# A hybrid decoder block on one core: half of w_out split earlier, the last unit's o written into loaded tiles, a wait of VectorE, and a new layout of the projection's input

## The chip, the cores and the metric

The kernel runs on one core of one Trainium2 chip. The metric is the device time of one execution in microseconds; lower is better. Several runs are made, and their median is given.

## The reference, cut to what matters

One layer, sequence 1024, model width 1024, everything in float32:

```python
mod = silu(c) @ w_ada + b_ada                      # six vectors of 1024: shift, scale, gate, twice
h = rms_norm(x, g_attn_pre) * (1 + sc_a) + sh_a
proj = h @ w_in
qa, ka, qb, kb = partial_rope(...)                 # parts of proj; va, vb without it
oa = banded_attention(qa, ka, va, 127, sink)       # 8 query heads, 2 key heads, width 64
ob = dilated_mixture_attention(qb, kb, vb)         # 8 heads; windows (128,1), (512,4), (2048,16)
mixed = concat(rms_norm(oa, g_mix_a), rms_norm(ob, g_mix_b))
x = x + gt_a * rms_norm(mixed @ w_out, g_attn_post)
h = rms_norm(x, g_mlp_pre) * (1 + sc_m) + sh_m
x = x + gt_m * rms_norm(square(relu(h @ w_up)) @ w_down, g_mlp_post)    # width 4096
```

## The kernel before

**Precision.** Every operand of a large matmul is split into a high part (float32r, made by a ScalarE copy) and a low part (the difference, made by VectorE or GpSimd). A product is three matmuls: high by high, high by low, low by high. A step of a product (128 deep, 512 wide) is therefore three lines of matmuls in the profile.

**Stages.** First the modulation and the normalised, transposed input h^T, which is split into the tile `hw`, of shape [128, 8, 2, 1024]: 8 slots, 2 parts (high, low), 1024 columns. Then six units of projection (`proj_tile`, `proj_mm`, L866 to L869; unit 0 in `first_unit` with its own order, the tiles are then called `acc`): units 0 and 1 are the two key groups of mixer A, units 2 to 5 two heads of mixer B each. A unit has two halves x of 512 tokens and three column groups c; each of these 36 tiles is 8 steps over k. `evac` rotates and splits q and k into staging tiles named `hl` and stores them by DMA into `qt` and `kt`. Beside the projection runs attention over 48 items (`emit_item`): for units 0 and 1 one item for each of 8 query blocks, for units 2 to 5 one for each of 4 pairs of query blocks (tp) and each of two heads. An item is scores (`s_ps`), a masked minimum on VectorE, an exponential on ScalarE, a scaling on GpSimd (L1158), transposes (`pt_ps`), a split (`ph`) and the product with v (`o_ps`). Its o goes through `otmp` and `ot` (L1294, L1298) to DRAM (`o_dram`, L1301).

**Output projection.** `load_wo` loads the eight 128-row pieces of w_out into staging tiles `wo_st` and splits them into the slots of `hw`, which the projection's input has left: ScalarE the high part (L1353), VectorE (L1356) or GpSimd (L1361 and L1362) the low one. A slot holds all k of one block of 128 tokens, so slots 0 to 3 are free after the last tile of half 0 (u = 5, x = 0, c = 2), and slots 4 to 7 after the very last projection tile. `open_out` then gives the memory of the projection's pools to a ring `ring_l`. `out_block(tb)` handles 128 tokens: it loads o (`o_sb`, L1423) when all items of its pair are stored, splits it (`oh`, `ol`), forms the two norms, multiplies by w_out (`y_ps`, L1478 to L1480; 16 steps of three matmuls), norms, gates, adds x (loaded at L1427) and stores the residual stream (`x_dram`). A second norm follows (`norm(2, e)`: VectorE L1515, GpSimd's power L1517, ScalarE L1532), then the transposes `px` (L1541) and their copies into `h2` with the modulation (L1557, L1560). `norm(0, e)` is the first norm of the block, with the same code. x can be loaded only once attention's pools have been closed (`open_h2`).

**MLP.** From the blocks of `h2`, w_up and w_down are multiplied in halves by a scheme with seven products where eight would be usual. Sums and differences of quarters are made by VectorE, and every operand is split by ScalarE and VectorE (L1669, L1676). Its matmuls are L1912 to L1914.

**What sets the order of the work.** The program is written out by a planner in the kernel, `Sched`. Every operation has an engine, an estimated duration, events that it depends on and resources that it takes and gives (`Res`: counts of free buffers, such as `r_stg` for five staging tiles, `r_wo` for the free slots of `hw`). `Sched.run` always emits the operation that could start first by these estimates; `prio` breaks ties, and for TensorE a list of preferences does (attention ahead of `dense` work, once the projections are done). The result is one fixed order for each engine and one for SP's DMA queue. On the chip each engine keeps to its order and waits on semaphores, whatever the true durations are. `feed_...` functions hand work to the planner when a condition holds: `feed_out` hands over block tb when 42 + 2 * (tb // 2) items of attention are done and at most ten steps of dense work are queued. `st.d` counts units of projection done.

## Time and profile before

| | us |
|---|---|
| median of 3 runs | 1146.05 |
| lowest and highest run | 1145.21, 1146.7 |
| the profiled execution, its own time | 1144.1 |
| its span, first to last instruction | 1142.2 |
| TensorE busy in it | 1113.5 (97%) |
| VectorE, ScalarE, GpSimd busy | 819.3, 636.1, 267.8 |

The profiled execution is a run of its own, and its time is not among the three. PE is TensorE's matmuls, PEld its weight loads, DVE VectorE, ACT ScalarE, POOL GpSimd, SP the queue that issues the DMAs. A row of a timeline gives the start and the duration in us, engine, line, operation, tiles (written <- read), shape, count, and in brackets the idle time of the engine before it with what ended it. Matmuls overlap, so their pace is read from their starts. "Granted clock" is the share of TensorE's full clock.

### The profile page before, as it was taken

Reading aid. Unit: us, or ns where it says so; the run is one execution under the profiler, and the core shown is the slowest. Engines: PE = TensorE matmul, PEld = TensorE weight load, DVE = VectorE, ACT = ScalarE, POOL = GpSimd, SP = SyncE. Lnnn points to the kernel's source line nnn. Section 1 sums busy time; section 2 is a strip of 40 time slices with the busy share of each in tenths; the row PEclk is TensorE's granted clock in tenths of the full one; section 3 lists DMA queues with packets and bytes.
Section 4 is the critical chain, followed back from the end, with each engine's and each line's share of the span. In section 5 each row is a group of like instructions: output and inputs, shape, how many; then the busy total and the mean of one; then the engine's idle time right before and its main releaser. Section 6 shows DMA issues by size and latency. Waiting matters only on the chain.

```text
span 1142.2 us, 15600 instructions
## 1 busy us (share of the span) xinstructions
PE 1113.5 (97%) x5417; PEld 925.2 (81%) x5417; DVE 819.3 (72%) x1378; ACT 636.1 (56%) x1101; POOL 267.8 (23%) x349
## 2 busy tenths in 40 slices
PE   8999999999999899998999999999999999999996
PEld 7788878888888687887888888888888888888885
DVE  7878666666667766668879664599644896537998
ACT  8868865464556755676675434553244733246542
POOL 2458867565743521112000000000000000000002
PEclk9999999999999899999999999999999999999998
DMA  9565545343423305555780168712469112584103
GB/s 351 187 208 164 164 155 168 136 155 125 141 77 133 127 26 186 185 202 217 284 310 19 56 230 292 280 41 70 152 245 331 55 56 86 202 304 164 37 19 148
DMA packets 90910, 185.29 MB, mean 162 GB/s; under 512 B 8400, under 2 KB 31056, under 8 KB 90832
## 3 DMA queue, kind: packets, MB, share of 16 engines
q1 hardware_dynamic: 90832, 184.30, 46.1%
q8 instruction: 43, 0.70, 0.2%
q14 instruction: 35, 0.29, 0.1%
HBM read 137.08 MB, written 28.31 MB: 145 GB/s over the span
## 4 chain that ended last, share of the span: by engine, by line
PE 77%; DVE 8%; ACT 4%; issue 4%; POOL 3%; DMA 3%; SPq 0%; DVEq 0%; POOLq 0%; ACTq 0%
PE mlp_ps L1913 17%; PE mlp_ps L1914 17%; PE mlp_ps L1912 17%; PE pj L866 4%; PE pj L869 4%; PE pj L867 4%; PE s_ps L1127 3%; PE o_ps L1262 2%; PE y_ps L1478 1%; PE pt_ps L1232 1%; PE y_ps L1479 1%; PE y_ps L1480 1%; PE pt_ps L1235 1%; DMA o_sb<-o_dram 1%; PE o_ps L1267 1%
## 5 line engine op out<-in xcount | busy, mean ns | idle before, releaser
L1912 PE MATMUL mlp_ps<-hw 128*128 128x512 f32 x896 | 349.8, 390 | 0.0
L1913 PE MATMUL mlp_ps<-hw 128*128 128x512 f32 x896 | 348.8, 389 | 0.0
L1914 PE MATMUL mlp_ps<-hw 128*128 128x512 f32 x896 | 348.8, 389 | 0.0
L1912 PEld LDWEIGHTS mlp_ps<-hw 128*128 128x128 f32 x896 | 168.5, 188 | 35.5 <-issue 0.5
L1913 PEld LDWEIGHTS mlp_ps<-hw 128*128 128x128 f32 x896 | 168.4, 188 | 35.2 <-issue 0.5
L1914 PEld LDWEIGHTS mlp_ps<-hw 128*128 128x128 f32 x896 | 168.4, 188 | 34.9
L1676 DVE TENSOR_TENSOR hw<-w,hw 128x1024 fp32r<-128x1024 f32 x96 | 114.7, 1222 | 95.5 <-ACT hw L1669 95.2
L1669 ACT CAST hw<-w 128x1024 fp32r<-128x1024 f32 x96 | 97.7, 1047 | 128.1 <-PE mlp_ps L1914 97.5
L2012 POOL TENSOR_TENSOR st<-st,nhalf 128x1 f32<-128x1 f32 x8 | 7.8, 977 | 598.5 <-DVE st L2010 598.5
L866 PE MATMUL pj<-hw,w_hl 128*128 128x512 f32 x240 | 102.9, 429 | 0.0
L869 PE MATMUL pj<-hw,w_hl 128*128 128x512 f32 x240 | 95.1, 396 | 0.0
L867 PE MATMUL pj<-hw,w_hl 128*128 128x512 f32 x240 | 94.9, 395 | 0.0
L1250 DVE TENSOR_TENSOR ph<-pt_ps,ph 128x512 fp32r<-128x512 f32 (+1 forms) x110 | 69.5, 648 | 32.9 <-ACT ph L1246 32.6
L1669 ACT CAST hw<-u 128x1024 fp32r<-128x1024 f32 x48 | 48.6, 1051 | 64.6 <-PE mlp_ps L1914 64.6
L1246 ACT CAST ph<-pt_ps 128x512 fp32r<-128x512 f32 (+1 forms) x110 | 59.0, 556 | 31.2 <-PE pt_ps L1235 26.1
L1153 ACT ACTIVATE p_sb<-p_sb,mn 128x128 f32<-128x128 f32 (+3 forms) x64 | 49.7, 777 | 38.7 <-DVE mn L1146 37.2
L1676 DVE TENSOR_TENSOR hw<-u,hw 128x1024 fp32r<-128x1024 f32 x48 | 57.1, 1221 | 18.2 <-ACT hw L1669 18.2
L1970 DVE TENSOR_TENSOR yacc<-yacc,mlp_ps 128x512 f32<-128x512 f32 x96 | 62.3, 685 | 3.3 <-PE mlp_ps L1914 3.3
L1158 POOL TENSOR_SCALAR p_sb<-p_sb,den 128x128 f32<-128x128 f32 (+3 forms) x64 | 48.6, 765 | 55.4 <-DVE den L1156 50.8
L1015 POOL TENSOR_TENSOR ada_acc<-ada_acc,wa_st 128x512 f32<-128x512 f32 x42 | 54.9, 1307 | 3.5
L869 PEld LDWEIGHTS pj<-hw,w_hl 128*128 128x128 f32 x240 | 45.4, 189 | 10.6
L1478 PE MATMUL y_ps<-hw,oh 128*128 128x512 f32 x128 | 52.0, 406 | 0.0
(206 smaller groups left out, 2015.8 us busy)
## 6 DMA issues: line engine op xcount, KB each, us to landing
hw<-s_dram SPq DMA_DIRECT2D x84, 512.0 KB, 4.2
wa_st<-in_w_ada SPq DMA_DIRECT2D x32, 512.0 KB, 4.3
w<-in_w_up SPq DMA_DIRECT2D x32, 512.0 KB, 4.9
w<-in_w_down SPq DMA_DIRECT2D x32, 512.0 KB, 7.0
s_dram<-hw SPq DMA_DIRECT2D x28, 512.0 KB, 3.4
qt<-hl SPq DMA_DIRECT2D x40, 256.0 KB, 2.6
w_st<-in_w_in SPq DMA_DIRECT2D x36, 256.0 KB, 2.9
x_sb<-in_x SPq DMA_DIRECT2D x16, 512.0 KB, 6.5
```

The source lines that it names most:

```text
L866: T.matmul(ps, w[:, 0, n], h[0], start=(k == 0), stop=False)
L867: T.matmul(ps, w[:, 1, n], h[0], start=False, stop=False)
L869: T.matmul(ps, w[:, 0, n], h[1], start=False, stop=(k == KC - 1))
L1246: A.copy(b["ph"][:, 0, :w], b["pt"][:, :w])
L1250: V.tensor_tensor(b["ph"][:, 1, :w], b["pt"][:, :w], b["ph"][:, 0, :w].bitcast(F32), ALU.subtract)
L1478: T.matmul(ps[:], b["oh"][:, k], wh[:, c0:c0 + 512], start=(k == 4 * m), stop=False)
L1669: A.copy(out[j][0], flat(src[j]))
L1676: V.tensor_tensor(out[j][1], flat(src[j]), out[j][0].bitcast(F32), ALU.subtract)
L1912: T.matmul(ps[m][:], sh, mh, start=starts and k == 0, stop=False, **kw)
L1913: T.matmul(ps[m][:], sh, ml_, start=False, stop=False, **kw)
L1914: T.matmul(ps[m][:], sl, mh, start=False, stop=k == 3, **kw)
L1970: e = op("DVE", t_dv(512), lambda: V.tensor_tensor(y(), y(), ps[m][:], ALU.add), [e, ml.e_y[tb, n]], gives=gives, prio=1)
```

## The change

Five edits:

- **Layout of `hw` in the projection** (`mod_chunk`, `proj_mm`): slot 4 * x + k // 2 holds the two k of a pair for the 512 tokens of half x, side by side. The moving operand of a projection matmul is then 512 elements in a row; before it was four pieces of 128 from four slots. The last tile of each half gives back one slot after each second k (`r_wo`, 1), not all four at its end.
- **Half of w_out split earlier** (`split_wo`, `feed_wo`): pieces k = 4 to 7 are loaded, split by ScalarE and VectorE into two staging tiles and stored to DRAM (`wo_dram`) when the projection stands at 2.2, 3.0, 3.8 and 4.6 units. `load_wo` splits k = 0 to 3 as before, but with VectorE alone, and loads both parts of k = 4 to 7 from DRAM into `hw`, 1 MB in two DMAs for each slot that comes free.
- **The last unit's o of blocks 0 and 1** (`open_out`, `t_pv`, `out_block`): seven of the eight o rows of both blocks are loaded as soon as `ring_l` is open, and VectorE writes the o of items (5, 0, 0) and (5, 0, 1) into the eighth row of these tiles, in two operations of 64x128 for each item. These two items are no longer stored to DRAM.
- **VectorE waits** (`norm`): for the second norm of the last block, the mean on VectorE, GpSimd's power and a copy of its result by VectorE are one operation of the planner on VectorE, so VectorE stands still until the power is done. For the blocks before the last two the planner's estimate of the power is 0.55 us, not 1.2.
- **Queue** (`feed_out`): a block is handed over when at most 17 steps of dense work are queued, not 10. `t.a` becomes the dictionary `h2` itself, so that quarters that are made later are found in it.

```diff
--- before.py
+++ after.py
@@ -677,8 +677,8 @@
     def mod_chunk(k, eg, half):
         t0, t1 = (0, TB) if half is None else (4 * half, 4 * half + 4)
         n = (t1 - t0) * P
-        ks = slice(k * P, (k + 1) * P)
-        h, hh = xnT[:, k, t0 * P:t1 * P].rearrange("p (b t) -> p b t", t=P), hw[:, t0:t1, 0, ks]
+        h = xnT[:, k, t0 * P:t1 * P].rearrange("p (x t) -> p x t", t=512)
+        hh, hl = (hw[:, t0 // 4 * 4 + k // 2:t1 - 3 + k // 2:4, i, k % 2 * 512:k % 2 * 512 + 512] for i in range(2))
         deps = [eg] + (e_xn[0] + e_xn[1] if half is None else e_xn[half])
 
         def full(eng):
@@ -689,7 +689,7 @@
         eh = op("ACT", t_sb(n) + 2 * AP_COST, lambda: A.activation(hh, h, AF.Identity, bias=s_a[:, k:k + 1],
                                                                   scale=g_a[:, k:k + 1]), deps, prio=0)
         e = op("ACT", t_sb(n) + 2 * AP_COST, full(A), [eh], prio=0)
-        e = op("DVE", t_dv(n), lambda: V.tensor_tensor(hw[:, t0:t1, 1, ks], h, hh.bitcast(F32), ALU.subtract), [e],
+        e = op("DVE", t_dv(n), lambda: V.tensor_tensor(hl, h, hh.bitcast(F32), ALU.subtract), [e],
                prio=0)
         for x in (0, 1) if half is None else (half,):
             e_hh[k, x], e_hl[k, x] = eh, e
@@ -858,10 +858,9 @@
 
     def proj_mm(ps, u, c, k, x, part):
         i, n = w_at(u, c, k)
-        t, w = slice(k * P, (k + 1) * P), w_hl[u, i]
-        n = slice(n * P, n * P + P)
-        h = [hw[:, 4 * x:4 * x + 4, i, t] for i in range(2)]
-        ps = ps[:].rearrange("p (b t) -> p b t", t=P)
+        w, n = w_hl[u, i], slice(n * P, n * P + P)
+        h = [hw[:, 4 * x + k // 2, i, k % 2 * 512:k % 2 * 512 + 512] for i in range(2)]
+        ps = ps[:]
         if part != 1:
             T.matmul(ps, w[:, 0, n], h[0], start=(k == 0), stop=False)
             T.matmul(ps, w[:, 1, n], h[0], start=False, stop=False)
@@ -927,8 +926,8 @@
             gives = []
             if x and k % 4 == 3:
                 gives.append((r_w, 1))
-            if u == 5 and c == 2 and k == KC - 1:
-                gives.append((r_wo, 4))
+            if u == 5 and c == 2 and k % 2:
+                gives.append((r_wo, 1))
             d = dense(0.681, emit, [w_e[u, w_at(u, c, k)[0]]], takes=[(r_pj, 1)] if k == 0 else [], gives=gives, after=tick)
         evac(u, x, c, lambda: b[0], d, r_pj)
 
@@ -1072,6 +1071,10 @@
         return ada.i == NADA
 
 
+    NSTG2 = 4
+    ph2 = Tok()
+    ph2.ot, ph2.e_ot, ph2.e_lo = {}, [Ev(), Ev()], {}
+
     items = [(u, qb) for u in range(2) for qb in range(TB)]
     items += [(u, tp, h) for u in range(2, 6)
               for tp, h in ((0, 0), (0, 1), (1, 0), (1, 1), (2, 0), *(((3, 0), (2, 1)) if u < 5 else ((2, 1), (3, 0))), (3, 1))]
@@ -1297,6 +1300,13 @@
                 ob["ot"] = opool.tile([64, 512], F32, name="ot", tag="ot")[:, :256]
                 V.tensor_tensor(ob["ot"][:], rec.o[0:64, :256], ob["tmp"][:, :256], ALU.add)
             e = op("ACT", t_ps(256), f_o1, [ep], takes=[(r_tmp, 1)], prio=0)
+            if (u, tp) == (5, 0):
+                def f_o3():
+                    for j in range(2):
+                        c = slice(P * j, P * j + P)
+                        V.tensor_tensor(ph2.ot[j][64 * h:64 * h + 64, KC - 1], rec.o[0:64, c], ob["tmp"][:, c], ALU.add)
+                e_o[i] = op("DVE", 2 * t_dv(P), f_o3, [e, *ph2.e_ot], gives=[(r_ob, 1), (r_tmp, 1)], prio=0)
+                return
             e = op("DVE", t_dv(256), f_o2, [e], takes=[(r_ot, 1)], gives=[(r_ob, 1), (r_tmp, 1)], prio=0)
             e_o[i] = load(lambda: nc.sync.dma_start(o_dram[tp][2 + u, 64 * h:64 * h + 64], ob["ot"][:]), 65536, [e],
                           gives=[(r_ot, 1)], prio=-5)
@@ -1333,16 +1343,46 @@
         return next_item[0] == len(items)
 
 
-    NSTG2 = 4
-    ph2 = Tok()
+    wo_dram = [[dram.tile([P, 1024], F32, name=f"wo_dram{k}_{i}") for i in range(2)] for k in range(4, KC)]
+    e_wod = {}
+
+    def split_wo(k):
+
+        raw, hi = [], []
+        g = cols[:, 56 + k:57 + k]
+
+        def f_l():
+            raw.append(stage("wo_st"))
+            nc.sync.dma_start(raw[0][:], w_out[k * P:(k + 1) * P])
+        e = load(f_l, 524288, takes=[(r_stg, 1)], prio=21)
+
+        def f_h():
+            hi.append(stage("wo_hi"))
+            A.mul(hi[0][:].bitcast(F32R), raw[0][:], g)
+        eh = op("ACT", t_sb(D) + AP_COST, f_h, [e], takes=[(r_stg, 1)], prio=9)
+
+        def f_lo():
+            V.scalar_tensor_tensor(raw[0][:].bitcast(F32R), raw[0][:], g, hi[0][:], ALU.mult, ALU.subtract)
+        el = op("DVE", t_dv(D) + AP_DV, f_lo, [eh], prio=9)
+        e_wod[k] = [load(lambda t=t, i=i: nc.sync.dma_start(wo_dram[k - 4][i][:], t[0][:]), 524288, [e_],
+                         gives=[(r_stg, 1)], prio=22) for i, (t, e_) in enumerate(((hi, eh), (raw, el)))]
+
+    def feed_wo():
+        k = 4 + len(e_wod)
+        if st.d > WO_AT[k - 4]:
+            split_wo(k)
+        return len(e_wod) == 4
+
+    WO_AT = (2.2, 3.0, 3.8, 4.6)
+    sc.launch.append(feed_wo)
 
     def load_wo():
 
-        if len(todo_dense) > 2 or ada.i < NADA:
+        if len(todo_dense) > 2 or ada.i < NADA or len(e_wod) < 4:
             return False
         ph2.e_wo, ph2.raw = {}, {}
         eh = None
-        for k in range(KC):
+        for k in range(4):
             def f_l(k=k):
                 ph2.raw[k] = stage("wo_st")
                 nc.sync.dma_start(ph2.raw[k][:], w_out[k * P:(k + 1) * P])
@@ -1356,12 +1396,12 @@
                 V.scalar_tensor_tensor(hw[:, k, 1], ph2.raw[k][:], g, hw[:, k, 0].bitcast(F32), ALU.mult,
                                        ALU.subtract)
             eh = op("ACT", t_sb(D) + AP_COST, f_h, [e] + ([eh] if eh else []), prio=4)
-
-            def f_lo2(k=k, g=g):
-                G.tensor_scalar(ph2.raw[k][:], ph2.raw[k][:], g, 1.0, ALU.mult, ALU.mult)
-                G.tensor_tensor(hw[:, k, 1], ph2.raw[k][:], hw[:, k, 0].bitcast(F32), ALU.subtract)
-            ph2.e_wo[k] = op(("DVE", "POOL"), (t_dv(D) + AP_DV, t_pts(D) + t_ptt(D)), (f_lo, f_lo2), [eh],
-                             gives=[(r_stg, 1)], prio=4)
+            ph2.e_wo[k] = op("DVE", t_dv(D) + AP_DV, f_lo, [eh], gives=[(r_stg, 1)], prio=4)
+        for k in range(4, KC):
+            def f_d(k=k):
+                for i in range(2):
+                    nc.sync.dma_start(hw[:, k, i].bitcast(F32), wo_dram[k - 4][i][:])
+            ph2.e_wo[k] = load(f_d, 1048576, e_wod[k], takes=[(r_wo, 1)], prio=-8, n=2)
         return True
 
     def open_out():
@@ -1375,6 +1415,14 @@
         ph2.r_o, ph2.r_y, ph2.r_tmp, ph2.r_xn = Res(2), Res(2), Res(1), Res(1)
         ph2.gate = ring_l("gate_a", F32)
         ph2.e_gate = load(lambda: nc.sync.dma_start(ph2.gate[:], gate_d[0][:]), 524288, [e_mod[0], e_mod[1]], prio=-7)
+        for tb in range(2):
+            def f_lo(tb=tb):
+                ph2.ot[tb] = by_k(ring_l("o_sb", F32))
+                nc.sync.dma_start(ph2.ot[tb][:, 0:KC - 1],
+                                  o_dram[0][0:KC - 1, :, tb * P:tb * P + P].rearrange("c p t -> p c t"))
+                ph2.e_ot[tb].t = 0.0
+            ph2.e_lo[tb] = load(f_lo, 458752, [e_ for k_, e_ in e_o.items() if near_o(k_, 0) and items[k_][0] < 5],
+                                takes=[(ph2.r_o, 1)], prio=-6)
         ph2.junk = pool("junk2", 1).tile([P, D], BF16, name="junk2")
         ph2.tb = 0
         sc.launch.append(feed_out)
@@ -1398,7 +1446,7 @@
 
     def feed_out():
         tb = ph2.tb
-        if tb < TB and st.att >= 42 + 2 * (tb // 2) and len(sc.pe.get("dense", [])) <= 10:
+        if tb < TB and st.att >= 42 + 2 * (tb // 2) and len(sc.pe.get("dense", [])) <= 17:
             out_block(tb)
             ph2.tb += 1
         return ph2.tb == TB
@@ -1413,6 +1461,9 @@
         i = pairs.pop(0)
         return i, (hw[:, i, 0], hw[:, i, 1])
 
+    def near_o(k, tp):
+        return (items[k][1] if items[k][0] > 1 else items[k][1] // 2) == tp
+
     def out_block(tb):
         b = {}
 
@@ -1425,16 +1476,20 @@
         def f_lx():
             b["xt"] = stage("x_sb2")
             nc.sync.dma_start(b["xt"][:], x[tb * P:(tb + 1) * P])
-        deps = [e_ for k_, e_ in e_o.items()
-                if (items[k_][1] if items[k_][0] > 1 else items[k_][1] // 2) == tb // 2]
-        el = load(f_lo, 524288, deps, takes=[(ph2.r_o, 1)], prio=-6)
+        deps = [e_ for k_, e_ in e_o.items() if near_o(k_, tb // 2)]
+        if tb < 2:
+            el = [ph2.e_lo[tb]] + deps
+        else:
+            el = [load(f_lo, 524288, deps, takes=[(ph2.r_o, 1)], prio=-6)]
         ex = load(f_lx, 524288, takes=[(r_stg, 1)], prio=-3)
 
         def f_oh():
             b["oh"] = by_k(ring_l("oh"))
             b["ol"] = by_k(ring_l("ol"))
+            if tb < 2:
+                b["ot"] = ph2.ot[tb]
             A.copy(b["oh"], b["ot"])
-        eh = op("ACT", t_sb(D), f_oh, [el], takes=[(ph2.r_ow, 2)], prio=2)
+        eh = op("ACT", t_sb(D), f_oh, el, takes=[(ph2.r_ow, 2)], prio=2)
 
         eo = op("DVE", t_dv(D), lambda: V.tensor_tensor(b["ol"], b["ot"], b["oh"].bitcast(F32), ALU.subtract), [eh],
                 prio=2)
@@ -1513,9 +1568,17 @@
                 t = small.tile([P, 8], F32, name="rs_t", tag="rs_t")
                 bx.append(t)
                 V.tensor_scalar(t[:, :1], b["st"][:, col:col + 1], 1.0 / D, EPS, ALU.mult, ALU.add)
-            e = op("DVE", 0.08, f1, [dep], prio=0)
-            return op("POOL", 1.2, lambda: G.tensor_tensor(b["st"][:, col + 1:col + 2], bx[0][:, :1], nhalf[:, :1],
-                                                            ALU.pow), [e], prio=0)
+            def f2():
+                G.tensor_tensor(b["st"][:, col + 1:col + 2], bx[0][:, :1], nhalf[:, :1], ALU.pow)
+            if tb < TB - 1 or col == 0:
+                e = op("DVE", 0.08, f1, [dep], prio=0)
+                return op("POOL", 0.55 if tb < TB - 2 else 1.2, f2, [e], prio=0)
+
+            def f3():
+                f1()
+                f2()
+                V.tensor_copy(bx[0][:, 1:2], b["st"][:, col + 1:col + 2])
+            return op("DVE", 0.95, f3, [dep], prio=0)
         e = op("ACT", t_sb(D) + AP_COST, f_sq(0, True), ey, prio=1)
         e = norm(0, e)
         e = op("DVE", t_dv(D), lambda: V.scalar_tensor_tensor(b["y"][:], b["y"][:], b["st"][:, 1:2], ph2.gate[:],
@@ -1720,7 +1783,7 @@
             fr.update({"T1": joins(r_raw, 2), "T3": joins(r_raw, 1), "B22": joins(r_raw, 3), "T4": joins(r_raw, 1),
                        "T2": joins(r_raw, 2)})
             if h == 0:
-                t.a = {q: h2[q] for q in h2}
+                t.a = h2
                 t.e_a = dict(e_h2)
                 t.ring = r_h2
                 t.new = ring_r
```

## The prediction

> **What bounds the kernel now.** I read the page first, then busy time by stretches, then the timelines of the engines around the two stretches in which TensorE is not full.
>
> ```profile
> span 1142.2 us, 15600 instructions
> PE 1113.5 (97%) x5417; PEld 925.2 (81%) x5417; DVE 819.3 (72%) x1378; ACT 636.1 (56%) x1101; POOL 267.8 (23%) x349
> ```
>
> TensorE is busy for 1113.5 of 1142.2 us. The change takes away no matmul, so it can only win TensorE's 28.7 us of idle time, the time lost at a lower clock, and a little pace. The next rows are busy time by stretches (two answers): stretch, length, busy time of PE, PEld, DVE, ACT and POOL, then the granted clock, DMA share and GB/s.
>
> ```profile
> 376.90:397.90 21.00, 16.30 (x93) 13.72 (x91) 17.88 (x48) 17.62 (x35) 12.94 (x11) 0.86 0.30 99
> ```
> ```profile
> 530.00:540.00 10.00, 7.69 (x32) 6.59 (x33) 6.54 (x13) 7.60 (x14) 1.08 (x1) 0.83 0.16 64
> 540.00:550.00 10.00, 10.00 (x46) 8.29 (x45) 10.00 (x11) 5.14 (x7) 0.00 (x0) 1.00 0.83 338
> ```
>
> Between 376.9 us, when the last projection matmul has been issued, and 397.9 us, when the output projection starts, TensorE has only attention to do: it is idle for 21.00 - 16.30 = 4.7 us, and the clock of 0.86 costs another 0.14 x 21 = 2.9 us. Around 530 us it is idle for 2.3 us of ten, and the clock of 0.83 costs 1.7 us more. From 540 us on, in the MLP, it is full. These two stretches are where the change works.
>
> **Part A, the last block's second norm.** One instruction of GpSimd, a power on a 128x1 column, stands between the last block and the MLP. First an earlier block's power, then the last one's:
>
> ```profile
> 428.15 0.55 POOL L1517 TENSOR_TENSOR st<-rs_t,nhalf 128x1 f32<-128x1 f32 x1 [5.78 <-DVE rs_t L1515]
> ```
> ```profile
> 526.49 4.59 POOL L1517 TENSOR_TENSOR st<-rs_t,nhalf 128x1 f32<-128x1 f32 x1 [7.40 <-DVE rs_t L1515]
> ```
> VectorE, ScalarE and TensorE around the last one:
> ```profile
> 526.26 0.15 DVE L1515 TENSOR_SCALAR rs_t<-st 128x1 f32<-128x1 f32 x1
> 526.32 0.95 DVE L1801 TENSOR_TENSOR sum_S<-h,h 128x768 f32<-128x768 f32 x1
> ```
> ```profile
> 533.47 1.37 DVE L1560 TENSOR_SCALAR h<-px,g_m,s_m 128x128 f32<-128x128 f32 x4 [2.79 <-PE px L1541]
> ```
> ```profile
> 531.11 1.15 ACT L1532 ACTIVATE xn<-y_sb,st 128x1024 f32<-128x1024 f32 x1 [2.86 <-POOL st L1517]
> ```
> ```profile
> 532.31 1.97 PE L1541 MATMUL px<-head,xn 128*128 128x128 f32 x8 [2.91 <-ACT xn L1532]
> ```
>
> The same power takes 0.55 us at 428 us and 4.59 us at 526 us. In the second case VectorE runs two-operand steps from 526.32 until its pause begins at 533.47 - 2.79 = 530.68, and GpSimd ends 0.4 us after that. The change lets VectorE write the mean, then wait for GpSimd and copy the result, so that none of those steps can start in between. Then the power ends near 526.41 + 0.1 + 0.55 = 527.1. xn (1.15 us on ScalarE, which stood idle for 2.86 us before 531.11, so from 528.25 at the latest) ends by 529.4, and the transposes can follow the last matmul, which ends at 532.31 - 2.91 = 529.40. All 2.91 us of idle time go, and with them the 1.7 us of low clock: at most 4.6. What waits behind VectorE's new wait is its queue of operand splits and sums; it loses about 0.75 us there, and gains the 2.79 us that it idled before 533.47, so TensorE should not feel it. If that cover failed, the wait would cost its 0.75. Bounds -4.6 to +0.75; I take -4.2, near the full end, since both rows of the power lie on this very instruction.
>
> **Part B, the start of the output projection.** TensorE, VectorE, GpSimd, SP's queue and ScalarE:
>
> ```profile
> 390.56 0.39 PE L1262 MATMUL o_ps<-ph,v_hl 128*128 128x256 f32 x1 [0.56 <-ACT ph L1246]
> 392.27 0.58 PE L1262 MATMUL o_ps<-ph,v_hl 128*128 128x256 f32 x1 [1.32 <-DVE ph L1250]
> ```
> ```profile
> 397.86 0.78 PE L1478 MATMUL y_ps<-hw,oh 128*128 128x512 f32 x1
> ```
> ```profile
> 386.99 0.41 DVE L1298 TENSOR_TENSOR ot<-o_ps,otmp 64x256 f32<-64x256 f32 x1
> ```
> ```profile
> 388.81 2.48 DVE L1356 SCALAR_TENSOR_TENSOR hw<-wo_st,head,hw 128x1024 fp32r<-128x1024 f32 x1
> ```
> ```profile
> 392.36 2.38 POOL L1362 TENSOR_TENSOR hw<-wo_st,hw 128x1024 fp32r<-128x1024 f32 x1
> 394.71 1.69 POOL L1158 TENSOR_SCALAR p_sb<-p_sb,den 128x640 f32<-128x640 f32 x2
> ```
> ```profile
> 391.75 0.38 SPq L1423 DMA_DIRECT2D o_sb<-o_dram  x1
> ```
> ```profile
> 396.32 1.05 ACT L1436 CAST oh<-o_sb 128x1024 fp32r<-128x1024 f32 x1 [0.55 <-DMA o_sb<-o_dram]
> ```
>
> The second half of w_out (k = 4 to 7) is split here, while attention needs the same engines: the wait of 1.32 us is for a VectorE step queued behind the split at 388.81, and the softmax scaling at 394.71 follows straight on GpSimd's part of a split. The o of block 0 is complete at 386.99 + 0.41 = 387.4, but goes to DRAM and back (its load is issued at 391.75), and its conversion starts at 396.32, 8.9 us later; matmuls follow 1.5 us after that. In the changed kernel these four splits are done long before and only loaded, and o goes straight into the tile. How early the loads can be (the last projection matmul, two groups of DMA issues with their us to landing, and the stretch with the most traffic):
>
> ```profile
> 376.65 0.40 PE L869 MATMUL pj<-hw,w_hl 128*128 128x512 f32 x1
> ```
> ```profile
> wo_st<-in_w_out SPq DMA_DIRECT2D x8, 512.0 KB, 5.1
> o_sb<-o_dram SPq DMA_DIRECT2D x8, 512.0 KB, 5.0
> ```
> ```profile
> 10.00:20.00 10.00, 9.10 (x60) 7.43 (x59) 8.44 (x15) 8.98 (x17) 2.00 (x4) 1.00 1.05 408
> ```
>
> The four slots come free during the last tile, the first some 4 us ahead of 376.65. Eight loads of 0.5 MB, the gate's 0.5 and twice 0.46 are 5.4 MB, 13.3 us at 408 GB/s. With about 2 us for the last to land they end near 388, or near 392 if they start only after the last matmul, and that is about when o is there. So I put the conversion at 389.5 and the first matmul at 391, 7 us before 397.86. Of the 7.6 us lost in the stretch, the two waits quoted (1.9) and the 2.9 of clock, which I put down to them, lie behind 390: 4.8. The other 2.8 are attention's own chain, and stay. I keep 0.8 of the 4.8 as still lost. Bounds -7.6 (all gone) to 0 (the loads land as late as o does now); I take -4.0. VectorE's two writes of 64x128 in place of one of 64x256 cost at most another 0.41 us in each of two chains; two stores on SP's queue are gone. Both are taken at nothing: TensorE's 2.8 us of waits in that chain are kept in full above.
>
> The rows show the clock low where waits of 1.32 and 2.91 us stand, and at 1.00 in the full stretches. "TensorE: Matmul & The Clock Gate" of the Trainium skill, Part 1, says that the clock halves after an idle window of about 3.4 us and returns after a busy one of that length. The trace differs: no wait quoted here is that long, and the clock is lower all the same. By that rule these gaps would not be what lowers the clock, and closing them would not bring it back: the third rival below.
>
> **Part C, between the blocks.**
>
> ```profile
> 418.07 0.39 PE L1262 MATMUL o_ps<-ph,v_hl 128*128 128x256 f32 x1 [0.49 <-DVE ph L1250]
> ```
> ```profile
> 439.13 1.09 PE L1541 MATMUL px<-head,xn 128*128 128x128 f32 x8 [1.51 <-ACT xn L1532]
> ```
> ```profile
> 429.40 0.58 SPq L1427 DMA_DIRECT2D x_sb<-in_x  x1
> ```
>
> The 0.49 us stand behind block 1's conversion, which the early load moves: -0.5 (0 to -0.5). The 1.51 us hang on the x rows, loaded at 429.40 when attention's buffers close; this order stays, and so do they. Emitting blocks at 17 queued steps in place of 10 lengthens the queue ahead of TensorE; no wait quoted is for an empty queue there, so it is worth nothing.
>
> **Part D, the layout of the projection's input.** The moving operand becomes 512 elements in a row, instead of four pieces of 128. Steps of the first unit, then of a later one, and one of the three lines:
>
> ```profile
> 59.41 0.39 PE L866 MATMUL acc<-hw,w_hl 128*128 128x512 f32 x1
> ...
> 67.11 0.39 PE L867 MATMUL acc<-hw,w_hl 128*128 128x512 f32 x1
> ```
> ```profile
> 354.00 0.39 PE L869 MATMUL pj<-hw,w_hl 128*128 128x512 f32 x1
> ...
> 356.06 0.40 PE L869 MATMUL pj<-hw,w_hl 128*128 128x512 f32 x1
> ```
> ```profile
> L867 PE MATMUL pj<-hw,w_hl 128*128 128x512 f32 x240 | 94.9, 395 | 0.0
> ```
>
> Thirty-four steps from 59.41 to 67.11 are 226.5 ns each, with the pieces; nine steps from 354.00 to 356.06 are 228.9. With three lines of 240 each, contiguity can give 720 x 2.4 ns = 1.7 us at most; since pieces also run at 226.5, perhaps nothing. I take -0.9.
>
> **Part E, what is added beside the projections.** Four times a load, a ScalarE and a VectorE pass and two stores, while units 2 to 4 are projected. ScalarE's price, then VectorE and TensorE at a stall, then two stretches:
>
> ```profile
> 351.03 2.18 ACT L1353 ACTIVATE hw<-wo_st,head 128x1024 fp32r<-128x1024 f32 x2
> ```
> ```profile
> 145.02 0.68 DVE L762 TENSOR_TENSOR hl<-pj,tab 64x512 f32<-64x512 f32 x1 [4.90 <-POOL ada_acc L1015]
> ```
> ```profile
> 148.79 0.74 PE L1182 MATMUL s_ps<-kt,qt 128*128 128x256 f32 x4 [1.80 <-DVE mn L1197]
> ```
> ```profile
> 140.00:160.00 20.00, 18.20 (x92) 14.86 (x91) 12.09 (x33) 11.60 (x33) 12.72 (x22) 0.91 0.45 143
> ```
> ```profile
> 150.00:310.00 160.00, 159.15 (x890) 134.12 (x889) 106.91 (x275) 90.58 (x205) 103.19 (x116) 0.99 0.46 151
> ```
>
> That is 4 x 1.1 us of ScalarE and at most 4 x 2.48 of VectorE (388.81 again), in 160 us in which they are busy for 90.6 and 106.9: hidden by the projection's matmuls. Three more issues each pass through SP's queue, ahead of q and k stores. The danger is the ring of five staging buffers: each split takes two. At 145.02 VectorE had waited 4.90 us for GpSimd to be done with such a buffer, and TensorE lost 1.80 us at 148.79 and 0.09 x 20 = 1.8 to the clock: 3.6 for one such stall. None costs 0, one per split 14.4. I take +1.0, near the low end, as TensorE lost only 0.85 us of idle time in the 160 us.
>
> **The sum.** -4.2 - 4.0 - 0.5 - 0.9 + 1.0 = -8.6 us. The profiled execution took 1144.1 us (span 1142.2 and 1.9 around it), so it would take 1135.5. The median of the runs is 1146.05, 1.95 above the profiled one; I take the same change there: 1137.5 us. The low ends of the parts give -4.6 - 7.6 - 0.5 - 1.7 = -14.4, and half of A and B with E at 1.0 about -3: 1131.6 to 1143 for this case alone.
>
> **The rivals.** *Slower, by the staging ring:* splits hold two of five buffers through a load, two passes and a store; the rotation of q and k waits as at 145.02, and with it scores and TensorE. For it speaks that row; against it, that the splits are spread over 140 us and that TensorE is full there. With the 1.0 of E replaced, three stalls of 3.6 bring the sum to +1.2, four to +4.8: from four on it is slower, 1150.9 us. *Part B is moved, not saved:* dense work starts at 391 but is used up before the x rows come after attention; B and C go, -4.1, so 1142 us. For it speaks the wait of 1.51 us at 439, where that already happens; against it, that attention too should end sooner. *The clock is not tied to the gaps:* 1.7 of A and 1.7 of B stay, -5.2, so 1140.8 us; against it, that the two stretches with a low clock here are those with the gaps. *It doesn't do what it says:* the order, written from estimates, puts VectorE's wait or the loads where they don't help, and gains and costs cancel: 1146 us.
>
> **How the numbers follow.** Forecast 0.46, part B moved 0.18, clock 0.05: faster, 0.69. Cancelled, 0.09: within 0.2%, which is 2.3 us and about what a measurement of this kernel can tell from no change. Staging ring, 0.22: slower. The range from 1131 to 1149 us takes in the forecast's own, the milder cases and the lower part of the slower one (two or three stalls); about 0.2 stay outside.
>
> **What would show it.** A: the last power under 1 us, no wait of TensorE over 0.5 us ahead of the last px, and a clock near 1.0 there. B: the first y_ps near 391 us, no split on GpSimd after 376 us, a clock over 0.95 until 400 us. D: nine projection steps in 2.04 us. E: no wait of VectorE over 2 us for a staging buffer. The prediction is wrong if new waits of over 3 us in all appear on TensorE between 150 and 376 us, or if the first y_ps doesn't come before 395 us.

## The result, and the profile after

The changed kernel takes 1138.63 us, median of 7 runs (1137.32 to 1143.56); the kernel before took 1145.41 us in the runs beside it. The ratio is 0.995, 95% interval 0.9937 to 0.9963: 6.8 us faster, where 8.6 were forecast. Measured a second time it took 1138.11 against 1144.1 us, ratio 0.9948 (0.9935 to 0.996): 6.0 us. The forecast of 1137.5 us is off by about a microsecond, but its gain was 1.8 to 2.6 us too large. Part of that closeness is luck: the forecast started from 1146.05 us, and the kernel before was 0.6 and 2.0 us quicker in the runs beside the change.

The first profiled execution of the changed kernel happens to be the longest of its seven runs (1143.56 us), so a second one, of 1137.57 us, is read beside it. Their pages, first and second:

```profile
span 1141.8 us, 15637 instructions
PE 1112.8 (97%) x5417; PEld 922.1 (81%) x5417; DVE 820.2 (72%) x1379; ACT 635.8 (56%) x1103; POOL 251.5 (22%) x346
```
```profile
span 1135.8 us, 15637 instructions
PE 1108.7 (98%) x5417; PEld 918.8 (81%) x5417; DVE 818.7 (72%) x1379; ACT 635.6 (56%) x1103; POOL 253.6 (22%) x346
```

They answer to 1142.2 us, PE 1113.5 and POOL 267.8 before. GpSimd lost its splits. Where the time went is seen by cutting the spans at the same matmuls (us):

| stretch | before | changed, 1st | changed, 2nd |
|---|---|---|---|
| to the first `acc` matmul | 22.9 | 23.9 | 23.9 |
| projections, to the end of the last `pj` | 354.1 | 360.8 | 354.8 |
| from there to the first `y_ps` | 20.8 | 14.5 | 14.5 |
| first to last `y_ps` | 117.1 | 118.8 | 118.8 |
| to the MLP's 337th matmul | 82.4 | 78.6 | 78.6 |
| the rest | 545.0 | 545.2 | 545.2 |

Parts B and C show in rows three and four, part A in row five, part E in row two. The first row varies: of all the profiles in this study that of the kernel before has the quickest start, and a kernel with an edit near 528 us alone begins at 24.4. So 1.0 us of its advantage is no cost of the change. Busy time by stretches, first and second profile (columns as before; clock third from the end):

```profile
145.00:160.00 15.00, 12.18 (x57) 9.07 (x56) 7.38 (x19) 7.44 (x17) 9.76 (x14) 0.89 0.54 165
350.00:384.60 34.60, 32.50 (x182) 27.52 (x181) 23.34 (x55) 19.38 (x38) 6.85 (x9) 0.95 0.39 146
384.60:399.20 14.60, 12.71 (x85) 10.87 (x83) 12.84 (x41) 11.34 (x27) 3.32 (x5) 1.00 0.81 299
525.00:535.00 10.00, 10.00 (x49) 8.17 (x48) 9.34 (x14) 7.58 (x13) 0.55 (x1) 1.00 0.30 120
```
```profile
145.00:160.00 15.00, 12.13 (x63) 9.09 (x61) 7.68 (x18) 8.02 (x18) 9.51 (x15) 1.00 0.56 180
350.00:378.60 28.60, 28.60 (x170) 24.74 (x171) 21.12 (x54) 16.65 (x34) 8.10 (x9) 1.00 0.34 122
378.60:393.20 14.60, 12.73 (x85) 10.88 (x84) 12.86 (x41) 11.34 (x26) 3.30 (x5) 1.00 0.81 296
```

Between the projections and the output projection 1.9 us are idle where 4.7 were, and the clock is 1.00 where it was 0.86. Around the last norm nothing is idle and the clock is 1.00, where 2.3 were idle at 0.83. GpSimd's power, VectorE beside it and the transposes behind it, in the first profile:

```profile
529.98 0.55 POOL L1572 TENSOR_TENSOR st<-rs_t,nhalf 128x1 f32<-128x1 f32 x1 [7.39 <-DVE rs_t L1570]
```
```profile
529.76 0.15 DVE L1570 TENSOR_SCALAR rs_t<-st 128x1 f32<-128x1 f32 x1
530.57 0.15 DVE L1580 COPY rs_t<-st 128x1 f32<-128x1 f32 x1 [0.66 <-POOL st L1572]
```
```profile
532.58 1.09 PE L1604 MATMUL px<-head,xn 128*128 128x128 f32 x8
```

The power takes 0.55 us in place of 4.59, VectorE stands for 0.66 us, and the 2.91 us ahead of `px` are gone.

What was not foreseen is in the projections. ScalarE and TensorE, first profile, then both for the second:

```profile
149.79 1.15 ACT L1361 ACTIVATE wo_hi<-wo_st,head 128x1024 fp32r<-128x1024 f32 x1 [4.93 <-DMA wo_st<-in_w_out]
351.83 1.15 ACT L1393 ACTIVATE hw<-wo_st,head 128x1024 fp32r<-128x1024 f32 x1 [4.28 <-DMA wo_st<-in_w_out]
```
```profile
152.72 0.50 PE L1277 MATMUL o_ps<-ph,v_hl 128*128 128x512 f32 x1 [2.59 <-ACT ph L1249]
354.38 0.66 PE L836 MATMUL pv<-head,vt 128*128 128x128 f32 x4 [2.10 <-ACT vt L830]
```
```profile
149.24 1.15 ACT L1361 ACTIVATE wo_hi<-wo_st,head 128x1024 fp32r<-128x1024 f32 x1 [4.75 <-DMA wo_st<-in_w_out]
347.37 1.15 ACT L1393 ACTIVATE hw<-wo_st,head 128x1024 fp32r<-128x1024 f32 x1 [2.16 <-DMA wo_st<-in_w_out]
```
```profile
152.17 0.50 PE L1277 MATMUL o_ps<-ph,v_hl 128*128 128x512 f32 x1 [2.41 <-ACT ph L1249]
```

ScalarE keeps to its order. A split stands in it at a place where its load, issued only at 146.28 us in the first profile and 145.87 us in the second, has not landed, and what ScalarE does for attention waits behind it, and TensorE for that. Both executions have the wait at 150 us. The one at 352 us stands at 347 us in the second, is half as long there and costs TensorE nothing; in the first, the stretch from 350 to 384.6 us holds 2.1 us of idle time and a clock of 0.95.

Why the load is issued so late is on SP's queue. The second profile's wait for this issue and the issue itself, then the GpSimd step that ends the wait, and the same step in the kernel before:

```profile
SPq L1356 <- POOL ada_acc L1014: 5.7, 1, 5.7
```
```profile
145.87 0.35 SPq L1356 DMA_DIRECT2D wo_st<-in_w_out  x1
```
```profile
144.55 1.29 POOL L1014 TENSOR_TENSOR ada_acc<-ada_acc,wa_st 128x512 f32<-128x512 f32 x1
```
```profile
143.69 1.29 POOL L1015 TENSOR_TENSOR ada_acc<-ada_acc,wa_st 128x512 f32<-128x512 f32 x1
```

GpSimd's step gives a staging buffer back. In the kernel before VectorE waits 4.90 us for that buffer (until 145.02 us); in the changed kernel the load of the first split waits for it, and ScalarE for the load. So the ring of five staging buffers is where both stalls come from.

### The profile page after: what moved, and what is told of

Same layout as the page of the kernel before. It is cut to its first block, busy times and chain, and to the rows that moved or that the text cites. A ratio compares the mean times of both kernels' runs of the same rounds, so it can differ in the third digit from the quotient of the medians.

```text
span 1141.8 us, 15637 instructions
## 1 busy us (share of the span) xinstructions
PE 1112.8 (97%) x5417; PEld 922.1 (81%) x5417; DVE 820.2 (72%) x1379; ACT 635.8 (56%) x1103; POOL 251.5 (22%) x346
## 4 chain that ended last, share of the span: by engine, by line
PE 74%; DVE 9%; ACT 5%; DMA 4%; issue 4%; POOL 3%; SPq 1%; DVEq 0%; POOLq 0%; ACTq 0%
PE mlp_ps L1975 16%; PE mlp_ps L1977 16%; PE mlp_ps L1976 16%; PE pj L865 4%; PE pj L866 3%; PE pj L868 3%; PE s_ps L1130 3%; DMA wo_st<-in_w_out 2%; PE o_ps L1265 1%; PE y_ps L1533 1%; PE y_ps L1535 1%; PE y_ps L1534 1%; PE pt_ps L1235 1%; DVE hw L1739 1%; PE pt_ps L1238 1%
## 5 line engine op out<-in xcount | busy, mean ns | idle before, releaser
L866 PE MATMUL pj<-hw,w_hl 128*128 128x512 f32 x240 | 94.9, 395 | 0.0
```

Of the source, the lines that this page charges most:

```text
L866: T.matmul(ps, w[:, 1, n], h[0], start=False, stop=False)
```

## The experiments

Each was run beside the kernel before; the ratio is to that.

**The changed kernel again** (the second profile above).

> The changed kernel itself once more, for a second profile and a second interval. In its first profile part E costs much more than predicted: the end of the projections comes 7.6 us later than before (384.69 against 377.05 us, 1.0 of it already in the first 24 us), because ScalarE, which works in order, stands 4.93 us at 149.8 us and 4.28 us at 351.8 us until a staged piece of w_out has landed. Theory L (these two waits hang on how late a load lands, so they differ from execution to execution): time near 1138.6 us, ratio 0.992 to 0.996, and the end of the projections 3 to 8 us later than before. Rival (the first profile was a mishap, and E costs nothing): the end of the projections within 1 us of before, and time near 1133 us, since B and A gave 6.3 and 3.8 us there.

1138.11 us (1137.48 to 1138.85), projections 0.7 us longer than before (1.6 later with the start). Theory L's time fits, its "3 to 8 us later" does not. The rival's "within 1 us" fits the projections without the start, its 1133 us does not: part of B is given back later (118.8 us of output projection against 117.1), and the start is 1.0 later. What E costs does vary between executions, by the second of the two waits and by the clock; the wait at 150 us is there in both.

**VectorE's wait alone.**

```diff
+            def f3():
+                f1()
+                f2()
+                V.tensor_copy(bx[0][:, 1:2], b["st"][:, col + 1:col + 2])
+            return op("DVE", 0.95, f3, [dep], prio=0)     # last block, second norm
```

> The kernel before with one edit: for the last block's second norm VectorE writes the mean, waits for GpSimd's power and copies its result, so that no two-operand step of VectorE runs beside the power. Theory A (the power is long only because VectorE works beside it, and nothing else holds the transposes back): the power takes about 0.55 us in place of 4.59, TensorE's idle of 2.91 us goes and the clock there is 1.00; time 3.8 to 4.6 us shorter, 1141 us, ratio 0.996 to 0.997. Rival (something else stands right behind it, or VectorE's waiting costs as much): time within 1 us of before, with a new wait ahead of the last transposes.

1139.58 us against 1144.1, ratio 0.996 (0.9945 to 0.9975): 4.5 us. The power, and the stretch around it:

```profile
528.03 0.54 POOL L1517 TENSOR_TENSOR st<-rs_t,nhalf 128x1 f32<-128x1 f32 x1 [7.40 <-DVE rs_t L1515]
```
```profile
523.00:533.00 10.00, 9.85 (x49) 7.96 (x48) 9.34 (x14) 7.39 (x12) 0.54 (x1) 1.00 0.31 127
```

From the last `y_ps` to the MLP's 337th matmul it is 78.2 us where it was 82.4. This is theory A, and most of what the whole change gains.

**The layout alone.**

```diff
-        h = [hw[:, 4 * x:4 * x + 4, i, t] for i in range(2)]
+        h = [hw[:, 4 * x + k // 2, i, k % 2 * 512:k % 2 * 512 + 512] for i in range(2)]
```

> The kernel before with the layout of the projection's input alone (512 elements in a row in place of four pieces of 128). In the two profiles the steps go at the same pace, 234.7 and 234.9 ns. Theory now: no effect, time within 1 us of before, ratio 0.999 to 1.001. Rival, the prediction's part D: 0.9 us shorter, at most 1.7, steps 2.4 ns faster.

1144.63 against 1144.1 us, ratio 1.0007 (0.9993 to 1.0021): no effect. One of the three lines in the groups by line. This file is one line shorter, so L866 here is L867 of the kernel before, where the mean was 395 ns:

```profile
L866 PE MATMUL pj<-hw,w_hl 128*128 128x512 f32 x240 | 94.5, 394 | 0.0
```

**One early split in place of four.**

```diff
-        return len(e_wod) == 4
+        return len(e_wod) == 1
-    WO_AT = (2.2, 3.0, 3.8, 4.6)
+    WO_AT = (4.6,)
-                    nc.sync.dma_start(hw[:, k, i].bitcast(F32), wo_dram[k - 4][i][:])
+                    nc.sync.dma_start(hw[:, k, i].bitcast(F32), wo_dram[0][i][:])
```

> The changed kernel with one early split in place of four (rows 512 to 639 of w_out, at the place of the last of the four); the eight loads of the split rows stay, all from that one piece. It leaves out the splits of rows 640 to 1023, so these rows are not used. Theory E (ScalarE's wait for a split's load is what the projections lose): the 4.9 us wait of ScalarE at 150 us goes with its split and the one at 352 us stays; 2 to 4 us shorter than the changed kernel, 1135 to 1136.5 us. Rival (splits beside the projections are free, and the later end of the projections has another cause, such as the order of the work or the first 24 us): within 1 us of the changed kernel.

This kernel leaves out three of the four splits and loads the one piece four times over. 1138.35 us (1135.9 to 1139.41): no faster, against theory E as I had put it. Its VectorE and TensorE say why:

```profile
145.95 0.69 DVE L762 TENSOR_TENSOR hl<-pj,tab 64x512 f32<-64x512 f32 x1 [4.85 <-POOL ada_acc L1014]
```
```profile
149.73 0.51 PE L1185 MATMUL s_ps<-kt,qt 128*128 128x256 f32 x2 [1.76 <-DVE mn L1200]
...
195.17 0.33 PE L836 MATMUL pv<-head,vt 128*128 128x128 f32 x1 [2.29 <-DVE ot L1301]
...
297.12 0.39 PE L1265 MATMUL o_ps<-ph,v_hl 128*128 128x256 f32 x1 [1.39 <-DVE ph L1253]
```

Without the split at 150 us the old stall is back: VectorE waits for a staging buffer as in the kernel before (4.90 us there). In the changed kernel that step of VectorE starts at 142 us without that wait. One wait has taken the other's place, both for the buffer that GpSimd gives back at 146 us, so the price of the early splits cannot be read from taking them away.

**The split's load told as late.** The planner counts the load of an early split as landing 6 us later (a wrapper that adds SLACK to the event's estimated time); ScalarE's split moves back in its order, and nothing else is edited.

```diff
-        eh = op("ACT", t_sb(D) + AP_COST, f_h, [e], takes=[(r_stg, 1)], prio=9)
+        eh = op("ACT", t_sb(D) + AP_COST, f_h, [Late(e, SLACK)], takes=[(r_stg, 1)], prio=9)
```

> The changed kernel, with the planner told that the load of an early split lands 6 us later than it estimates, so that it puts ScalarE's pass further back in ScalarE's order. In both profiles of the changed kernel the pass of the first split stands where ScalarE waits for its load (4.93 us in the first) and TensorE loses 2.4 to 2.6 us at 152 us. Theory L (that wait is a cost of the early split): ScalarE's wait goes, TensorE's idle at 152 us falls below 1 us, and the kernel is 2 to 3 us faster than the changed one, 1135.5 us. Rival (something is late there anyway: the kernel before, with no split, idles 1.80 us at 149 us, and the kernel with VectorE's wait alone 1.75 us): another wait takes its place, and the time stays within 1 us of the changed kernel.

1132.55 us, ratio 0.9891 (0.9874 to 0.9909): twice the gain expected. Run again on another chip:

> The kernel with the slack on the early splits, once more, on the chip of the three beside it, and for a second profile: 1131.5 to 1133.5 us again, with no idle time of TensorE over 0.5 us between 145 and 160 us. If its first time was a matter of chance, 1135 us or more, and the wait is back.

1132.91 us (1131.77 to 1133.15), ratio 0.9897 (0.9883 to 0.9911). Its stretch and its ScalarE:

```profile
145.00:160.00 15.00, 15.00 (x82) 12.31 (x81) 12.54 (x39) 11.94 (x33) 12.29 (x19) 1.00 0.72 231
```
```profile
145.13 0.62 ACT L768 CAST hl<-hl 128x512 fp32r<-128x512 f32 x1 [0.41 <-ACT tab L723]
...
150.39 1.14 ACT L1371 ACTIVATE wo_hi<-wo_st,head 128x1024 fp32r<-128x1024 f32 x1
```

The split of a q or k tile, which stood behind the wait and ended at 150.9 us in the second profile, now starts at 145.13, and the split at 150.39 waits for nothing. TensorE has no idle time in these 15 us. The load is no earlier: its issue still waits 5.7 us for the buffer, until 146.13 us. What has gone is both engines' waiting for it, the new wait and the old one.

**The slack for the first split alone** (`Late(e, SLACK if k == 4 else 0.0)`).

> The slack of 6 us for the first of the four early splits alone. Theory F (all of the gain is at 145 to 160 us, where ScalarE waited 4.75 us for this split's load and where TensorE now has no idle time): as fast as with the slack on all four, 1131.5 to 1134 us, and no idle time of TensorE over 0.5 us between 145 and 160 us. Rival (the order as a whole fell out better by chance, or the other splits matter): 1135 to 1138 us, with TensorE waiting at the other splits.

1133.59 us (1132.63 to 1136.53), ratio 0.991 (0.9895 to 0.9925), beside 1132.91 for all four; no wait over 0.25 us stands between 145 and 160 us. So theory F holds for nearly all of it: one place in one engine's order is worth 4.5 us (1138.11 to 1133.59). It is not E's price against the kernel before, which had a stall of its own at this place (1.80 us of TensorE's idle time).

**The slack for the last splits too** (4 us for the loads of k = 0 to 3 near 345 us).

> The slack of 6 us for the early splits, and one of 4 us for the loads of the four splits that are left near 345 us, where ScalarE waited 2.8 us with the slack on the early ones alone and TensorE idled 0.61 us. Theory (these waits too are ScalarE's order being written for loads that land late): ScalarE's wait there goes; up to 1 us faster, 1131.5 to 1132.5 us. Rival (the last splits are in the way of the end of the projections, and a later place delays the output projection): 1133 to 1136 us.

1129.39 us (1128.98 to 1129.54), ratio 0.9869 (0.9851 to 0.9886). The stretch around those splits with the slack on the early ones alone, and here:

```profile
335.00:350.00 15.00, 13.86 (x80) 11.60 (x79) 8.77 (x19) 9.96 (x16) 1.12 (x1) 1.00 0.57 203
```
```profile
335.00:350.00 15.00, 15.00 (x90) 12.93 (x90) 9.77 (x21) 10.25 (x17) 1.92 (x2) 1.00 0.56 194
```

1.1 us of idle time are gone, as expected. Another 2.0 came from the output projection, whose order fell out differently (below); that was not foreseen.

**o through DRAM again**, with the early splits kept (the two items are stored, and the blocks load o as the others do).

```diff
-            if (u, tp) == (5, 0):
+            if False:
-        if tb < 2:
+        if False:
             el = [ph2.e_lo[tb]] + deps
```

> The changed kernel without the direct write of o: the last unit's o of the first two blocks goes to DRAM and back as before; the early splits and their loads stay. Theory O (the way of o through DRAM holds the first output matmul): the first y_ps comes 4 us or more later, 18 us or more after the last projection matmul in place of 14.5, and the time grows by 1 to 4 us. Rival S (the late splits were what held it): the first y_ps stays within 1.5 us, and the time within 1 us of the changed kernel.

1136.85 us, ratio 0.9926 (0.9906 to 0.9946, which overlaps the changed kernel's): not slower, though its first `y_ps` comes 18.8 us after the projections in place of 14.5. Both theories fall: the direct o does bring the first matmul 4.3 us forward, and that is worth nothing at the end. With the slack:

> The slack of 6 us for the early splits, and o through DRAM again in place of the direct write. Without the slack, o through DRAM was 1.3 us faster (1136.85 against 1138.1 us), though its first y_ps came 4.3 us later after the last projection matmul. Theory M (output matmuls that start earlier are used up before attention ends, so the direct o moves work and saves nothing): within 1.5 us of the kernel with slack alone, 1131 to 1133 us, with the first y_ps 18 to 19 us after the last projection matmul. Rival (the direct o is worth its 4.3 us once the projections no longer stall): 1135 to 1137 us.

1129.55 us (1128.05 to 1130.56), ratio 0.987 (0.9854 to 0.9886), beside 1132.91 with the direct o on the same chip: 3.4 us faster without it, and theory M does not go far enough. The stretch from the last `pj` to the last `y_ps` and the first transposes, first with the direct o, then through DRAM (both with the slack):

```profile
373.90:507.40 133.50, 127.86 (x673) 105.95 (x672) 90.36 (x189) 89.29 (x153) 23.61 (x34) 1.00 0.46 160
```
```profile
431.86 1.09 PE L1615 MATMUL px<-head,xn 128*128 128x128 f32 x8 [0.99 <-ACT xn L1606]
```
```profile
374.20:504.70 130.50, 127.10 (x673) 106.14 (x671) 90.61 (x187) 89.48 (x153) 23.77 (x34) 1.00 0.49 165
```
```profile
428.62 1.04 PE L1607 MATMUL px<-head,xn 128*128 128x128 f32 x8
```

The same 673 matmuls, with 5.6 us idle in the one and 3.4 in the other. With the direct o 55 output matmuls start before attention's last one has ended, 46.3 us after the projections; through DRAM it is 43, and attention ends after 43.0. What is used up beside attention is then missing ahead of `px`: all 96 matmuls of blocks 0 and 1 are done there, against 90. That wait is 1.0 us of the 2.2 us of idle time between the two; the rest is in shorter waits. With both slacks the direct o has no such wait (`px` at 428.50 us, 131.4 us for the stretch), which speaks for the order and not the write itself as what decides; that is not shown apart. Both slacks with o through DRAM were not tried.

**The queue at 10 steps** (`<= 17` back to `<= 10`).

> The changed kernel with blocks of the output projection emitted at 10 queued steps again, in place of 17. The prediction took this part for nothing: time within 1 us of the changed kernel. Rival (the longer queue is what lets output matmuls fill attention's waits): the first y_ps or the stretch up to the end of the output projection comes over 1 us later, and the time grows by 1 to 3 us.

1139.97 us (1137.35 to 1141.87), ratio 0.9961 (0.9948 to 0.9973), 14.5 us from the last `pj` to the first `y_ps` as with 17, and 0.6 us more to the last. Its interval overlaps that of the changed kernel: between nothing and 1.9 us, not settled.

**All splits late**, as before; the rest of the change kept (`load_wo` as in the kernel before, no `split_wo`).

> The changed kernel with all eight splits of w_out where they were before (beside the last attention, two of them partly on GpSimd), nothing of them early and nothing through DRAM; the direct o, the layout and VectorE's wait stay. Theory S (the splits beside attention held the first output matmul): it comes 18 us or more after the last projection matmul in place of 14.5, with a granted clock under 0.95 there, and the end of the output projection comes later too; less the price of the early splits, the time grows by 0.5 to 3 us. Rival O (the direct o alone brings it): the first y_ps stays within 1.5 us, and the kernel is as fast as the changed one or up to 1 us faster, as nothing is added beside the projections.

1140.09 us (1138.43 to 1141.8), ratio 0.9958 (0.9944 to 0.9972), by medians 1.5 us slower than the changed kernel in its first comparison and 2.0 in its second, though the intervals overlap. The first `y_ps` comes 16.6 us after the projections, between the bounds of the two theories, the clock is low again, and splits stand on GpSimd and VectorE as they did:

```profile
379.20:395.80 16.60, 12.36 (x69) 10.24 (x68) 14.06 (x34) 12.49 (x25) 7.94 (x6) 0.90 0.46 152
```
```profile
383.42 2.36 POOL L1369 TENSOR_TENSOR hw<-wo_st,hw 128x1024 fp32r<-128x1024 f32 x1
```

At the first `y_ps` theory S thus holds for 2.1 us of the 6.3, and the direct o brings the rest, 4.3 us by its own run. For the time, the early splits are worth 1.5 to 2 us after their price by medians, not settled. From the end of the projections to the last `y_ps` this kernel takes 134.5 us where the kernel before takes 137.9: beside late splits the direct o, the longer queue and slots that come free earlier do save something together. No run separates them.

## Why the prediction was right, and where it was wrong

The sign and the two largest terms were right; the sum was too large by 1.8 to 2.6 us.

- **A, -4.2 taken:** 4.5 us by the wait alone, 3.8 in both profiles of the whole change, every step as written: power, VectorE's pause, transposes, clock. The rival by which the clock is not tied to the gaps falls here: with the gap closed it is 1.00 in the 10 us in which it was 0.83, and with the layout alone, where the gap stays (2.93 us), it is 0.83 there again.
- **B and C, -4.5 taken:** from the end of the projections to the last `y_ps` it is 137.9 us before and 133.3 in both profiles: -4.6. The conversion starts 12.7 us after the last `pj` and the first `y_ps` 14.5, against 12.5 and 14 forecast (389.5 and 391 against 377.05). But 1.7 us of the 6.3 won there are given back by the last `y_ps`, and the runs through DRAM show that beside early splits the direct o could be left out. The sum was right for a partly wrong reason: the rival "moved, not saved" holds for the direct o there, and what is saved is the splits' disturbance and the clock. `px` still waits, 1.1 us. The 13.3 us for the loads take 0.5 MB for 524,288 bytes; with 5.6 MB in all it is 13.8, half a microsecond more, and the conversion came when it was forecast all the same.
- **D, -0.9 taken:** nothing. The bound "perhaps nothing" was written beside it, from steps with pieces that ran at the same pace, and should have been the value.
- **E, +1.0 taken:** the failed step. The ring of staging buffers was the right danger, but the prediction looked for the wait on VectorE and took ScalarE's passes as hidden. No wait of VectorE over 2 us for a staging buffer appeared; the load of the first split waited 5.7 us for one instead, and ScalarE stood 4.75 and 4.93 us in its order behind that load. The rival by the staging ring thus had the place, but the wait was one of a load and not of the rotation of q and k, and there was one such stall in place of four. In four profiles with the early splits at their place (the two of the changed kernel, the queue at 10, o through DRAM) the projections take 354.8 to 360.8 us; with one early split 356.5; in four without early splits 354.1 to 355.5; in the five with a slack 349.2 to 351.0. So E costs 0.7 to 6.7 us against the kernel before. The 0.7 may be lucky: TensorE is idle for 7.4 us of the projections there against 5.5 before, and the clock between 145 and 160 us is 1.00 against 0.89. In the second profile the rows of the table give -6.5 us: -4.6 for B and C, -3.8 for A, 0.7 for E, 1.0 for the start and 0.2 for the rest.
- **Its own tests:** "first `y_ps` before 395 us" failed in the first profile (399.20) and held in the second (393.18), though B was the same in both. It should have been set from the end of the projections. The other sign, new waits of over 3 us on TensorE between 150 and 376 us, appeared in both profiles, as the price of E: it waits 7.13 and 4.45 us there, against 0.95 in the kernel before. (The kernel before's stall of 1.80 us ends at 148.79, just ahead of that window.) So by the prediction's own sign its account of the projections was wrong, though its time came true.

## What to carry to other kernels

Where a planner writes a fixed order for each engine, a new step that depends on a DMA can be cheap in busy time and still hold back all that stands behind it; give its load a late estimate, and look at what the engine waits for at that place, and at what the load itself waited for (here a step of 1.15 us on ScalarE stood behind a load that waited for a buffer, and telling the planner 6 us more made the kernel 4.5 to 5.6 us faster). A stall that an edit removes can hide in a stall that it adds, so replace the wait rather than take the edit away when you want its price. The first matmul of a stage coming earlier is no gain if the stage ends by running out of work: count what is left where the next wait stands.

The best versions run here are the change with both slacks, 1129.39 us, and that with the early slack and o through DRAM, 1129.55 us: by their medians some 14.5 us faster than the kernel before beside them, and 8.6 us below the change. The intervals of the two overlap.

## What the runs showed of the hardware that was not expected

GpSimd's power of one column takes 0.54 and 0.55 us where VectorE stands still, and 4.59 us (526.49 to 531.08) where VectorE runs two-operand steps. In the kernel before these go on, behind the one at 526.32, until 530.68:

```profile
527.19 2.36 DVE L1676 TENSOR_TENSOR hw<-w,hw 128x1024 fp32r<-128x1024 f32 x2
529.46 1.22 DVE L1843 TENSOR_TENSOR sum_T<-w,w 128x1024 f32<-128x1024 f32 x1
```

It fits "SBUF — State Buffer" of the Trainium skill, "SBUF: two separate sides", by which the two engines share a pair of ports that one holds for a whole instruction while the other is blocked. But the power is held up through four steps here, not one; why it does not get its turn between them, no run here shows.

Whether the clock falls after a short gap differs between executions. Two stretches behind gaps of 1.80 us (the kernel before, 148.79 us) and 2.59 us (the changed kernel, first profile):

```profile
151.00:153.00 2.00, 2.00 (x7) 1.54 (x6) 1.28 (x5) 1.24 (x6) 0.46 (x2) 0.50 0.40 119
```
```profile
156.00:158.00 2.00, 2.00 (x8) 1.61 (x7) 0.52 (x2) 0.66 (x2) 1.30 (x4) 0.54 0.94 151
```

Behind gaps of 1.75 us (VectorE's wait alone, 150.19 us) and 2.41 us (the changed kernel, second profile) it stays:

```profile
152.00:154.00 2.00, 2.00 (x10) 1.44 (x8) 1.68 (x5) 2.00 (x9) 0.31 (x2) 1.00 0.25 66
```
```profile
154.00:156.00 2.00, 2.00 (x11) 1.39 (x10) 1.87 (x3) 1.65 (x6) 0.78 (x2) 1.00 0.50 133
```

Over 15 us a clock of 0.89 takes up to 1.65 us besides such a gap. So a wait can cost nearly twice its length in one execution and its own length in another; the length of a gap alone does not tell which. The loss need not reach the end of a stage: with the layout alone the clock stayed at 1.00 behind the stall at 150 us, and the projections took 354.1 us as in the kernel before.
